# A hybrid decoder layer: six of eleven blocks of the second down pair by seven products, two of them made behind the next block's first

## The chip, the cores and the metric

One core of one Trainium2 chip runs the whole kernel in one launch. The metric is device time in microseconds, the median of several executions. One execution was also taken by the hardware profiler; all rows quoted below are from it. Engines: PE is TensorE, DVE is VectorE, ACT is ScalarE, POOL is GpSimd, SP is SyncE, which here only issues DMAs.

## The reference

One layer of a decoder for 256 rows of 2048 channels. Only its last step matters here:

```
def hybrid_layer(x, g_mix, w_in, ..., w_gu, w_down, rel_bias):
    ...                                    # three attention branches, merged with gates
    x = x + merged @ w_out
    h2 = rmsnorm(x, g_ffn)
    gu = h2 @ w_gu
    x = x + (jax.nn.silu(gu[..., :D_FF]) * gu[..., D_FF:]) @ w_down
    return x
```

All values are float32. With D_FF = 5632 the down projection multiplies a (256 x 5632) activation by a (5632 x 2048) weight.

## The kernel before

Each float32 operand of a large product is split into a high part (rounded to the matmul's format, `fp32r`, by a cast on ACT) and a low part (what is left, by a subtraction on DVE); the product is three matmuls, high by high, high by low and low by high (`product`, lines 177 to 179; the split is line 109, in `split`, called by `parts`). One weight tile is a "quarter" of 512 KB: 128 partitions x 2 k-tiles x 512 columns. Its split parts go into the tiles `w_hi` and `w_lo`, of which there are five each; a sixth cast must wait until PE is done with the first.

The down projection is made in two pairs of column blocks, 2 x 512 columns each, by `down_pair`. The second call, whose code changes, makes the last 1024 columns. In a pair the inner dimension is eleven blocks of 512. A block is a 2 x 2 matrix (two halves of rows of the activation, t, and two halves of the inner dimension, kh) times a 2 x 2 matrix of quarters (kh, n), and it is made in one of two ways:

- plainly (`rest`, one quarter a step): four quarters, each split once, 12 matmuls of 128x512 a quarter, 48 in all;
- by seven products (`seven`) instead of eight, with sums of quarters: seven splits, six matmuls each, 42 in all. f1 multiplies b11; f5 multiplies u = b11 + b12; f6 multiplies u + b22; f7 multiplies b12 + b22; f3 is b22, f2 is b21; f4 multiplies u + b21. f1, f5, f6 and f7 collect in PSUM tiles of their own for all blocks of the pair, and `combine` adds them into the output at the end; f2, f3 and f4 go straight into the output tiles (`own`).

In the second pair of the kernel before, five blocks are made by sevens: 4, 6, 8, 3 and 5, in this order; six are plain. u is one buffer (`bufs=1`): b11 + b12 and then + b22 are adds on DVE (lines 1203 and 1207), and the + b21 is a DMA that adds, issued by POOL (line 1229); b12 + b22 is such a DMA too (line 1223). In the last block the + b21 is a DVE add (line 1227). Where `seven` yields True, the caller puts one plain step in (`rest`): four for each block, after f1, f5, f6 and f7. The last plain block closes the pair.

The activation's sums that a block by sevens needs exist for blocks 4, 6 and 8 from the first pair. For blocks 3 and 5, `sums_again` loads the activation once more through POOL's queue (line 1154), makes four sums on DVE (lines 231 to 236) and splits them into the room of a plain block that is done (`again = {0: 3, 1: 5}`).

The weights' loads are issued by SP in its program's order (line 319); `w_raw` has four buffers for plain steps, `g_raw` four for blocks by sevens. The order on each engine is set by a scheduler in the build, except where `keep_in_program_order` holds an instruction in the place in which the code has it. PSUM: the pair's tiles `z`, `v` and two of `tr` are the output's (`own`), `ps` and `qs` (two each) hold f1, f5, f6 and f7.

Of the kernel before, what the change touches and what calls it, by code (L numbers as in the profile page):

```python
# [10 lines left out]
F32 = mybir.dt.float32  # L11
# [3 lines left out]
ALU = mybir.AluOpType  # L15
# [4 lines left out]
P = 128  # L20
# [10 lines left out]
NB = 512  # L31
# [25 lines left out]
def hybrid_block(ctx: ExitStack, tc: tile.TileContext, x, w_in, w_branch, w_out, w_gu, w_down, rel_bias,  # L57
                 onehot, extra, across, factors, out):
    nc = tc.nc
# [22 lines left out]
    def pool(stack, name, side, bufs=1):  # L82
        return stack.enter_context(tc.tile_pool(name=name, bufs=bufs, side=side, reuse_waits="tile"))
# [31 lines left out]
    def block(w, k, col0):  # L115

        return w[col0 // NB, k // 2]
# [30 lines left out]
    def project(acts, k0, w, row0, nk, col0, ps=None, done=0, there=(), last=1):  # L148


        ps = ps or banks()
        held = []
        for k, w_hi, w_lo in weights(w, row0, done, nk, col0, there):
            if k:
                advance(stages)
            if k % 2 == 0 and k:
                advance(slow_stages)
            held.append((k, w_hi, w_lo))
            if k < nk - last or k == nk - 1:
                for t in range(NT):  # L160
                    for kk, hi, lo in held:
                        product(ps[t], *acts.plain(t, k0 + kk), hi, lo, kk == 0, kk == nk - 1)
                held = []
        return ps
# [75 lines left out]
    class Sums:  # L240
# [22 lines left out]
        def form(self, f, c, j):  # L263
            if f in SUM_AT:
                kh, t = SUM_AT[f]
                return [x[:, 2 * kh + j, t * P:(t + 1) * P] for x in self.s[c]]
            return self.plain(*{1: (0, 4 * c + j), 2: (0, 4 * c + 2 + j), 4: (1, 4 * c + 2 + j)}[f])
# [48 lines left out]
    def load(w, k, col0, pl=None):  # L316

        raw = pl.tile([P, 2, NB], F32, name="g_raw", bufs=6 if pl is gx else 4) if pl else wpool.tile([P, 2, NB], F32, name="w_raw", bufs=4)
        (nc.sync.dma_start if w is w_down else fetch)(raw, block(w, k, col0))
        return raw  # L320
# [25 lines left out]
    def quarter(acts, w, kh, col0):  # L346
        return [load(w, 4 * c + 2 * kh, col0, gx) for c in acts.wc]

    def begin_pair(acts, w, colA, colB):

        b11, b12 = (quarter(acts, w, 0, col0) for col0 in (colA, colB))
        p11 = [parts(b) for b in b11]
        u = [gx.tile([P, 2, NB], F32, name="u") for _ in acts.wc]
        for a, b, d in zip(b11, b12, u):
            nc.vector.tensor_add(d, a, b)  # L355
        b21 = quarter(acts, w, 1, colA)
        return p11, b12, u, b21, [parts(b) for b in (u if by_banks(w) else b21)]
# [515 lines left out]
    def gate_col(c, b):  # L873
        return 3 * NH * HD + b * D + c * NB

    def pair_of(kind, what):
        if kind == "qk":
            return hs, w_in, what * NB, NH * HD + what * NB
        if kind == "gates":
            return hs, w_in, gate_col(*what[0]), gate_col(*what[1])  # L880
        if kind == "vv":
            return hs, w_in, V0 + what[0] * NB, V0 + what[1] * NB
        if kind == "vg":
            return hs, w_in, V0 + what[0] * NB, gate_col(*what[1])
# [15 lines left out]
    ahead = None  # L900
    for (kind, what), after in zip(units, units[1:] + [(None, None)]):
# [9 lines left out]
        if kind in ("qk", "gates", "vv", "vg"):  # L911
            ps, ahead = project_pair(*pair_of(kind, what), ahead, nxt, others is in_turn)
            if others is in_turn:
                turn.reverse()
        else:
            ps = project(h, 0, w_in, 0, KT, V0 + what * NB if kind == "v" else gate_col(*what),
                         *((ps0, 4, there) if (kind, what) == ("v", 0) else ()))
            ahead = begin_pair(*nxt) if nxt else None
# [57 lines left out]
    for c in range(4):  # L976
        ms = [half_kb() for _ in range(NT)]
        for b, (k0, nk) in enumerate(((0, H_A), (H_A, H_B), (H_A + H_B, H_C))):
# [3 lines left out]
            ps = project(o, k0, w_branch, k0 * P, nk, c * NB)  # L982
            if (c, b) == (3, 2):
# [4 lines left out]
                ahead = begin_pair(ms_sums.part(WC[:1]), w_out, NB, 0)  # L988
# [38 lines left out]
    gd = pool(ctx, "gd", "right", 4)  # L1027
# [22 lines left out]
    WD = (4, 6, 8)  # L1050
# [81 lines left out]
    pd = pool(ctx, "pd", "left")  # L1132
# [30 lines left out]
    def down_pair(c0, mine, spare, queues, sevenths, again={}):  # L1163


        own = dict(zip(((0, 0), (1, 0), (0, 1), (1, 1)), mine()))
# [7 lines left out]
        def into(ps, lhs, wh, wl, last=False, half=None):  # L1174
            for j in range(2):
                product(ps, *lhs(j), wh[:, j], wl[:, j], id(ps) not in begun, last and j == 1, half)
                begun.add(id(ps))
# [12 lines left out]
        def form(ps, f, c, src, last=False):  # L1190
            wh, wl = parts(src)
            into(ps, lambda j: a.form(f, c, j), wh, wl, last)

        def seven(c, f1, f5, f6, f7, last):
            def quarter(kh, n):
                return load(w_down, 4 * c + 2 * kh, c0 + n * NB, gd)

            b11 = quarter(0, 0)
            form(f1, 1, c, b11, last)
            yield bool(again)  # L1200
            b12 = quarter(0, 1)
            u = gd.tile([P, 2, NB], F32, name="u", bufs=1)
            tc.keep_in_program_order(nc.vector.tensor_add(u, b11, b12))  # L1203
            form(f5, 5, c, u, last)
            yield bool(again)
            b22 = quarter(1, 1)
            nc.vector.tensor_add(u, u, b22)
            if not again:
                form(f6, 6, c, u, last)
                yield  # L1210
                nc.vector.tensor_add(b12, b12, b22)
                form(f7, 7, c, b12, last)
                yield
                form(own[0, 1], 3, c, b22)
                yield
                b21 = quarter(1, 0)
                form(own[0, 0], 2, c, b21)
                yield
                nc.vector.tensor_add(u, u, b21)
                form(own[1, 0], 4, c, u)  # L1220
                yield
                return
            nc.gpsimd.dma_start(b12, b22, accum_op=ALU.add)
            form(f6, 6, c, u, last)
            b21 = quarter(1, 0)
            if last:
                tc.keep_in_program_order(nc.vector.tensor_add(u, u, b21))
            else:
                nc.gpsimd.dma_start(u, b21, accum_op=ALU.add)
            yield True  # L1230
            form(own[0, 1], 3, c, b22)
            yield
            form(own[0, 0], 2, c, b21)
            yield
            form(f7, 7, c, b12, last)
            yield True
            form(own[1, 0], 4, c, u)
            yield

        def combine(f1, f5, f6, f7):  # L1240

# [14 lines left out]
        def by_sevens():  # L1256
            f = spare()
            apart.extend(f[:1] if again else ())
            for c in sevenths:
                yield from seven(c, *f, c == sevenths[-1])  # L1260
            yield from combine(*f)

        sevens = by_sevens()
# [34 lines left out]
        return [acc2.tile([P, NB], F32, name=n) for n in "zv"] + [tr.tile([P, NB], F32, name="tr") for _ in range(2)]  # L1298

    down_pair(0, in_acc, elsewhere, (nc.scalar, nc.gpsimd), WD)  # L1300
    down_pair(2 * NB, elsewhere, in_acc, (nc.sync, nc.scalar), WD + (3, 5), {0: 3, 1: 5})


_INS = ["x", "w_in", "w_branch", "w_out", "w_gu", "w_down", "rel_bias"]
# [33 lines left out]
```

## Time and profile before

| what | value |
|---|---|
| median of three runs | 1336.18 us (1335.87 to 1337.33) |
| the profiled execution | 1335.64 us |
| its span from the first to the last instruction | 1333.9 us |
| PE busy | 1327.6 us |
| DVE busy | 1176.0 us |
| ACT busy | 946.2 us |
| POOL busy | 132.4 us |
| DMA, mean over the span | 267 GB/s |

The profiled execution is the one that every duration below comes from; between its span and its time lie 1.7 us, and it stands 0.54 us under the median. PE shows as busy nearly throughout. A matmul's own record is longer (0.38 us) than the time to the next one's start, since matmuls are pipelined, so times between starts are what counts for PE, and the same holds for the records of ACT and DVE to a smaller degree. The second pair's matmuls begin at 1222.67 us of the span. In a timeline row the columns are: start, duration, engine, line, operation, output and inputs by the program's names, form, and in brackets the idle time of the engine before it with what ended it.

### The profile page before, as it was taken

The page shows a single profiled execution, that of the slowest core. Times are in us where ns is not written, and L with a number is a line of the kernel's source. Part 1 is how long each engine was busy: PE and PEld are TensorE (multiplying, and loading weights), DVE is VectorE, ACT ScalarE, POOL GpSimd, SP SyncE. Part 2 cuts the span into 40 slices and gives each one's busy share as a digit, 9 for nine tenths or more (in the row PEclk, how much of TensorE's full clock was granted, in tenths as well). Part 3 has the DMA queues.
Part 4 walks back from the last instruction along what each step waited for, and adds up shares of the span by engine and source line. Part 5 has one row for each costly group of instructions (what it writes and reads, how often), then busy time and mean ns, then how long its engine had stood idle before and what let it go on. Part 6 is the DMA issues. An engine that isn't in the chain of part 4 may idle for free.

```text
span 1333.9 us, 17798 instructions
## 1 busy us (share of the span) xinstructions
PE 1327.6 (100%) x6243; PEld 1158.4 (87%) x6243; DVE 1176.0 (88%) x1261; ACT 946.2 (71%) x1216; POOL 132.4 (10%) x197
## 2 busy tenths in 40 slices
PE   9999999999999999999999999999999999999998
PEld 6888888888888888888888888888888888888887
DVE  7978898989888897888999999998889997998887
ACT  6786867788777776546778778777877876665563
POOL 1100110001111111110210000001000001001010
PEclk9999999999999999999999999999999999999999
DMA  9987977897789878887988889889899977789893
GB/s 359 307 284 243 263 211 256 254 282 215 263 267 289 275 245 276 297 304 255 284 314 268 273 257 275 234 260 302 280 286 278 270 222 256 250 276 303 269 273 96
DMA packets 119793, 355.75 MB, mean 267 GB/s; under 512 B 32864, under 2 KB 34584, under 8 KB 119704
## 3 DMA queue, kind: packets, MB, share of 16 engines
q1 hardware_dynamic: 77016, 277.45, 57.9%
q0 software_dynamic: 20272, 70.81, 22.7%
q10 hardware_dynamic: 22416, 6.36, 3.0%
q8 instruction: 49, 0.80, 0.2%
q14 instruction: 40, 0.33, 0.1%
HBM read 294.26 MB, written 14.70 MB: 232 GB/s over the span
## 4 chain that ended last, share of the span: by engine, by line
PE 97%; DVE 1%; DMA 1%; ACT 0%; issue 0%; SPq 0%; DVEq 0%; ACTq 0%
PE qs L178 12%; PE qs L177 12%; PE qs L179 12%; PE ps L178 11%; PE ps L179 11%; PE ps L177 11%; PE z L177 4%; PE z L179 4%; PE z L178 4%; PE v L177 3%; PE v L179 3%; PE v L178 3%; PE tr L179 1%; PE tr L177 1%; PE tr L178 1%; PE tr L210 1%
## 5 line engine op out<-in xcount | busy, mean ns | idle before, releaser
L109 DVE TENSOR_TENSOR w_lo<-w_raw,w_hi 128x1024 fp32r<-128x1024 f32 x298 | 361.5, 1222 | 45.6 <-ACT w_hi L109 44.4
L109 ACT CAST w_hi<-w_raw 128x1024 fp32r<-128x1024 f32 x298 | 309.3, 1047 | 95.8 <-PE qs L179 26.0
L109 ACT CAST w_hi<-g_raw 128x1024 fp32r<-128x1024 f32 x220 | 227.0, 1050 | 105.7 <-PE qs L179 32.9
L109 DVE TENSOR_TENSOR w_lo<-g_raw,w_hi 128x1024 fp32r<-128x1024 f32 x220 | 262.7, 1223 | 19.4 <-ACT w_hi L109 16.9
L109 ACT CAST w_hi<-u 128x1024 fp32r<-128x1024 f32 x165 | 172.1, 1049 | 116.9 <-DVE u L1203 21.3
L109 DVE TENSOR_TENSOR w_lo<-u,w_hi 128x1024 fp32r<-128x1024 f32 x165 | 199.8, 1224 | 45.0 <-ACT w_hi L109 40.1
L178 PE MATMUL qs<-w_lo,h_hi 128*128 128x512 f32 x348 | 132.6, 381 | 0.0
L179 PE MATMUL qs<-w_hi,h_lo 128*128 128x512 f32 x348 | 132.1, 379 | 0.0
L178 PE MATMUL ps<-w_lo,h_hi 128*128 128x512 f32 x336 | 128.0, 381 | 0.5 <-DVE w_lo L109 0.5
L179 PE MATMUL ps<-w_hi,h_lo 128*128 128x512 f32 x336 | 127.4, 380 | 0.1
L177 PE MATMUL qs<-w_hi,h_hi 128*128 128x512 f32 x348 | 127.4, 382 | 0.0
L177 PE MATMUL ps<-w_hi,h_hi 128*128 128x512 f32 x336 | 123.1, 382 | 0.0
L406 POOL DMA_DIRECT2D u<-g_raw x47 | 40.9, 871 | 375.6 <-DVE w_lo L109 311.2
L177 PEld LDWEIGHTS qs<-w_hi,h_hi 128*128 128x128 f32 x348 | 65.7, 189 | 9.5 <-ACT sc L339 0.4
L178 PEld LDWEIGHTS qs<-w_lo,h_hi 128*128 128x128 f32 x348 | 65.8, 189 | 9.2
L179 PEld LDWEIGHTS qs<-w_hi,h_lo 128*128 128x128 f32 x348 | 65.8, 189 | 9.2
L178 PEld LDWEIGHTS ps<-w_lo,h_hi 128*128 128x128 f32 x336 | 63.5, 189 | 9.9 <-DVE w_lo L109 1.3
L179 PEld LDWEIGHTS ps<-w_hi,h_lo 128*128 128x128 f32 x336 | 63.5, 189 | 9.9 <-DVE h_lo L109 1.1
L177 PEld LDWEIGHTS ps<-w_hi,h_hi 128*128 128x128 f32 x336 | 63.3, 189 | 9.2 <-ACT h_hi L109 0.6
L355 DVE TENSOR_TENSOR u<-g_raw 128x1024 f32<-128x1024 f32 x47 | 57.4, 1223 | 10.3 <-DMA g_raw<-in_w_gu 7.6
L344 DVE TENSOR_TENSOR u<-u,g_raw 128x1024 f32<-128x1024 f32 x47 | 55.5, 1220 | 0.0
L400 POOL DMA_DIRECT2D g_raw<-g_raw x21 | 18.2, 865 | 255.5 <-DMA g_raw<-in_w_in 104.3
(442 smaller groups left out, 2982.3 us busy)
## 6 DMA issues: line engine op xcount, KB each, us to landing
w_raw<-in_w_in SPq DMA_DIRECT2D x103, 512.0 KB, 7.1
g_raw<-in_w_in SPq DMA_DIRECT2D x88, 512.0 KB, 6.1
g_raw<-in_w_gu SPq DMA_DIRECT2D x88, 512.0 KB, 6.1
w_raw<-in_w_gu SPq DMA_DIRECT2D x88, 512.0 KB, 6.5
w_raw<-in_w_down SPq DMA_DIRECT2D x56, 512.0 KB, 4.9
u<-g_raw POOLq DMA_DIRECT2D x51, 512.0 KB, 6.1
w_raw<-in_w_branch SPq DMA_DIRECT2D x32, 512.0 KB, 4.8
g_raw<-in_w_down SPq DMA_DIRECT2D x32, 512.0 KB, 5.1
```

The costliest lines, as they stand in the source:

```text
L109: cast, rest = nc.scalar.copy(hi, src), nc.vector.tensor_sub(lo, src, hi.bitcast(F32))
L177: nc.tensor.matmul(ps, ah, wh, start=start, stop=False, **how)
L178: nc.tensor.matmul(ps, ah, wl, start=False, stop=False, **how)
L179: nc.tensor.matmul(ps, al, wh, start=False, stop=stop, **how)
L210: nc.tensor.transpose(pt[:, i, :], src[:, i * P:(i + 1) * P], ident)
L344: tc.keep_in_program_order(nc.vector.tensor_add(d, d, a))
L355: nc.vector.tensor_add(d, a, b)
L400: nc.gpsimd.dma_start(d, a, accum_op=ALU.add)
L406: nc.gpsimd.dma_start(d, a, accum_op=ALU.add)
```

## The change

Block 7 joins the blocks made by sevens: 4, 6, 8, 3, 5, 7, so five blocks stay plain. Its activation sums are made again in the room of block 2. A new generator, `sevens_apart`, takes the place of `seven` in the second pair: f7 and f4 of a block are put off (`due`) and made right after f1 of the next block. For the third and the fifth of the six blocks (8 and 5), u and b12 stand not in their usual buffers but in the room of block 4's activation sums (`a_shi4`, `a_slo4`), which are read no more by then; b12 is loaded there directly (line 1241). The plain steps are placed anew: before f5 (`ahead`), before f6 (`amid`) and before f3 (`behind`), 16 in all: three each for blocks 4, 6, 8 and 3, and two each for blocks 5 (none before f3) and 7 (none before f5). The first block's u + b21 is now a DVE add, like the last one's.

```
-            yield bool(again)
...                                 (seven: the first pair's form alone stays)
+        def sevens_apart(f1, f5, f6, f7):
+            due = []
+            def quarter(c, kh, n):
+                return load(w_down, 4 * c + 2 * kh, c0 + n * NB, gd)
+            def overdue():
+                while due:
+                    ps, f, c, src, last = due.pop(0)
+                    form(ps, f, c, src, last)
+                    yield
+            for i, c in enumerate(sevenths):
+                last = c == sevenths[-1]
+                ahead, amid, behind = i < 5, True, i < 4 or last
+                b11 = quarter(c, 0, 0)
+                if i and i % 2 == 0:
+                    b12, u = (pd.tile([P, 2, NB], F32, name=f"a_s{n}{sevenths[0]}") for n in ("hi", "lo"))
+                    nc.sync.dma_start(b12, block(w_down, 4 * c, c0 + NB))
+                else:
+                    b12, u = quarter(c, 0, 1), gd.tile([P, 2, NB], F32, name="u", bufs=1)
+                form(f1, 1, c, b11, last)
+                yield
+                yield from overdue()
+                tc.keep_in_program_order(nc.vector.tensor_add(u, b11, b12))
+                yield ahead
+                form(f5, 5, c, u, last)
+                b22 = quarter(c, 1, 1)
+                tc.keep_in_program_order(nc.vector.tensor_add(u, u, b22))
+                nc.gpsimd.dma_start(b12, b22, accum_op=ALU.add)
+                yield amid
                 form(f6, 6, c, u, last)
+                b21 = quarter(c, 1, 0)
+                if i and not last:
+                    nc.gpsimd.dma_start(u, b21, accum_op=ALU.add)
+                yield behind
+                if last or not i:
+                    tc.keep_in_program_order(nc.vector.tensor_add(u, u, b21))
                 form(own[0, 1], 3, c, b22)
                 yield
                 form(own[0, 0], 2, c, b21)
                 yield
-            form(f7, 7, c, b12, last)
-            yield True
-            form(own[1, 0], 4, c, u)
-            yield
+                due += [(f7, 7, c, b12, last), (own[1, 0], 4, c, u, False)]
+                if last or not i:
+                    yield from overdue()
...
-            for c in sevenths:
-                yield from seven(c, *f, c == sevenths[-1])
+            if again:
+                yield from sevens_apart(*f)
+            else:
+                for c in sevenths:
+                    yield from seven(c, *f, c == sevenths[-1])
...
-    down_pair(2 * NB, elsewhere, in_acc, (nc.sync, nc.scalar), WD + (3, 5), {0: 3, 1: 5})
+    down_pair(2 * NB, elsewhere, in_acc, (nc.sync, nc.scalar), WD + (3, 5, 7), {0: 3, 1: 5, 2: 7})
```

Two places show how the order moves. The first is ACT's, from the cast for f6 of one block to the cast for f5 of the next. Before, between blocks 3 and 5: the casts are f6's (from u), a plain step's (`w_raw`), f3's, f2's, f7's (`g_raw` each), a plain step's, f4's (u), f1's of block 5, a plain step's, and f5's (the new u).

```order
L109 CAST w_hi_11742<-u_11708 128x1024
L109 CAST w_hi_11757<-w_raw_11755 128x1024
L109 CAST w_hi_11773<-g_raw_11738 128x1024
L109 CAST w_hi_11783<-g_raw_11752 128x1024
L109 CAST w_hi_11793<-g_raw_11706 128x1024
L109 CAST w_hi_11805<-w_raw_11803 128x1024
L109 CAST w_hi_11821<-u_11708 128x1024
L109 CAST w_hi_11833<-g_raw_11831 128x1024
L109 CAST w_hi_11845<-w_raw_11843 128x1024
L109 CAST w_hi_11865<-u_11863 128x1024
```

Now, between blocks 5 and 7: f6's (`a_slo4` is u here), f3's, f2's, f1's of block 7, f7's of block 5 (`a_shi4` is b12), f4's of block 5, the copy of the sum of f1, f5's of block 7, a plain step's, f6's of block 7.

```order
L109 CAST w_hi_11833<-a_slo4_11744 128x1024
L109 CAST w_hi_11846<-g_raw_11811 128x1024
L109 CAST w_hi_11856<-g_raw_11843 128x1024
L109 CAST w_hi_11871<-g_raw_11866 128x1024
L109 CAST w_hi_11881<-a_shi4_11743 128x1024
L109 CAST w_hi_11891<-a_slo4_11744 128x1024
L339 COPY sc_12005<-ps_11191 128x512
L109 CAST w_hi_11902<-u_11870 128x1024
L109 CAST w_hi_11918<-w_raw_11916 128x1024
L109 CAST w_hi_11934<-u_11870 128x1024
```

Three plain steps' casts that stood between f6's and the next f5's are gone, and f1 of the next block has moved ahead of f4.

The second place is DVE's, from the low part of f4 to that of the next block's f5. Before, between blocks 8 and 3: low parts of f4, of f1, of a plain step, then the add that makes the new u, then f5's low part.

```order
L109 TENSOR_TENSOR w_lo_11667<-u_11547,w_hi_11666 128x1024
L109 TENSOR_TENSOR w_lo_11679<-g_raw_11676,w_hi_11678 128x1024
L109 TENSOR_TENSOR w_lo_11691<-w_raw_11688,w_hi_11690 128x1024
L1203 TENSOR_TENSOR u_11708<-g_raw_11676,g_raw_11706 128x1024
L109 TENSOR_TENSOR w_lo_11711<-u_11708,w_hi_11710 128x1024
```

Now, between blocks 3 and 5: the low part of f4, then the four sums of `sums_again` for block 7 with a plain step's low part among them, then the add, the low part of the activation's sums and f5's low part.

```order
L109 TENSOR_TENSOR w_lo_11767<-u_11600,w_hi_11766 128x1024
L231 TENSOR_TENSOR a_raw_11723<-a_raw_11723 128x2x128
L109 TENSOR_TENSOR w_lo_11784<-w_raw_11781,w_hi_11783 128x1024
L234 TENSOR_TENSOR a_raw_11723<-a_raw_11723 128x2x128
L235 TENSOR_TENSOR a_raw_11723<-a_raw_11723 128x2x128
L236 TENSOR_TENSOR a_raw_11723<-a_raw_11723 128x2x128
L1247 TENSOR_TENSOR a_slo4_11744<-g_raw_11741,a_shi4_11743 128x1024
L109 TENSOR_TENSOR a_lo2_6423<-a_raw_11723,a_hi2_6422 128x1024
L109 TENSOR_TENSOR w_lo_11802<-a_slo4_11744,w_hi_11801 128x1024
```

f1's low part has moved ahead of f4's, and a set of sums has come between f4 and the new u.

More of the change, by code (lines that the diff above doesn't have):

```diff
@@ L1204, in seven @@
             form(f5, 5, c, u, last)
-            yield bool(again)
+            yield
             b22 = quarter(1, 1)
             nc.vector.tensor_add(u, u, b22)
-            if not again:
-                form(f6, 6, c, u, last)
-                yield
-                nc.vector.tensor_add(b12, b12, b22)
-                form(f7, 7, c, b12, last)
-                yield
+            form(f6, 6, c, u, last)
+            yield
+            nc.vector.tensor_add(b12, b12, b22)
+            form(f7, 7, c, b12, last)
@@ new lines, in seven @@
+            yield
+            form(own[0, 1], 3, c, b22)
+            yield
+            b21 = quarter(1, 0)
+            form(own[0, 0], 2, c, b21)
+            yield
+            nc.vector.tensor_add(u, u, b21)
+            form(own[1, 0], 4, c, u)
+            yield
+        def sevens_apart(f1, f5, f6, f7):
[6 more added lines that the diff above has]
+                    form(ps, f, c, src, last)
+                    yield
+            for i, c in enumerate(sevenths):
[8 more added lines that the diff above has]
+                form(f1, 1, c, b11, last)
+                yield
+                yield from overdue()
[6 more added lines that the diff above has]
+                yield amid
+                form(f6, 6, c, u, last)
+                b21 = quarter(c, 1, 0)
[4 more added lines that the diff above has]
+                    tc.keep_in_program_order(nc.vector.tensor_add(u, u, b21))
@@ L1214, in seven @@
                 form(own[0, 1], 3, c, b22)
                 yield
-                b21 = quarter(1, 0)
                 form(own[0, 0], 2, c, b21)
                 yield
-                nc.vector.tensor_add(u, u, b21)
-                form(own[1, 0], 4, c, u)
[L1221 to L1229, printed above, removed]
@@ L1230, in seven @@
-            yield True
[L1231 to L1238, printed above, removed]
+                due += [(f7, 7, c, b12, last), (own[1, 0], 4, c, u, False)]
+                if last or not i:
+                    yield from overdue()
         def combine(f1, f5, f6, f7):
```

## The prediction

> **What bounds the kernel now.** I read the page's busy shares and chain first, then the engines by stretch, then the order of time around the second down pair (PE there from 1222.67 us).
>
> ```profile
> span 1333.9 us, 17798 instructions
> PE 1327.6 (100%) x6243; PEld 1158.4 (87%) x6243; DVE 1176.0 (88%) x1261; ACT 946.2 (71%) x1216; POOL 132.4 (10%) x197
> PE 97%; DVE 1%; DMA 1%; ACT 0%; issue 0%; SPq 0%; DVEq 0%; ACTq 0%
> ...
> 1223.00:1320.00 97.00, 97.00 (x451) 84.94 (x450) 83.42 (x83) 58.66 (x59) 7.94 (x10) 1.00 0.81 244
> 1320.00:1334.00 14.00, 10.36 (x54) 9.05 (x52) 6.52 (x13) 0.00 (x0) 0.00 (x0) 0.99 0.22 76
> ...
> PE ps L178 <- DVE w_lo L109: 0.5, 2, 0.3
> ```
>
> The two stretch rows give length, then busy time of PE, PEld, DVE, ACT and POOL, the clock, the DMA share and GB/s. PE is busy for all 97.00 us of the pair's main stretch at full clock; the last row is its longest wait for a split, 0.3 us in one piece. So the kernel is bound by its matmuls, and fewer matmuls are worth their time as long as the splits stay ahead of PE. DVE (83.42 of 97 us) and the DMA engines (0.81) are close behind.
>
> How far ahead are they? Product names: f1 to f7 as in the code. PE, one block of the pair:
>
> ```profile
> 1265.41 0.38 PE L177 MATMUL ps<-w_hi,a_shi 128*128 128x512 f32 x1
> ...
> 1269.29 0.38 PE L177 MATMUL qs<-w_hi,a_shi 128*128 128x512 f32 x1
> ...
> 1279.65 0.38 PE L177 MATMUL v<-w_hi,a_1hi 128*128 128x512 f32 x1
> ...
> 1284.83 0.38 PE L177 MATMUL ps<-w_hi,hi 128*128 128x512 f32 x1
> ```
>
> These are the first matmuls of f5, f6 and f4 of block 8 and of f5 of block 3. From f5 to f5 lie 42 matmuls of a block and four plain steps of 12: 90 in 19.42 us, 0.2158 us each. Now the other side, which makes the operand that f5, f6 and f4 share (u): ACT, then DVE and POOL.
>
> ```profile
> 1260.32 1.05 ACT L109 CAST w_hi<-u 128x1024 fp32r<-128x1024 f32 x1 [2.51 <-DVE u L1203]
> ...
> 1265.35 1.05 ACT L109 CAST w_hi<-u 128x1024 fp32r<-128x1024 f32 x1 [3.04 <-DVE u L1207]
> ...
> 1273.96 1.06 ACT L109 CAST w_hi<-u 128x1024 fp32r<-128x1024 f32 x1 [1.69 <-DMA u<-g_raw]
> 1274.92 1.04 ACT L109 CAST w_hi<-g_raw 128x1024 fp32r<-128x1024 f32 x1
> 1276.18 1.05 ACT L109 CAST w_hi<-w_raw 128x1024 fp32r<-128x1024 f32 x1 [0.23 <-PE z L179]
> 1279.80 1.06 ACT L109 CAST w_hi<-u 128x1024 fp32r<-128x1024 f32 x1 [2.56 <-DVE u L1203]
> ...
> 1284.49 1.05 ACT L109 CAST w_hi<-u 128x1024 fp32r<-128x1024 f32 x1 [2.71 <-DVE u L1207]
> 1285.44 1.04 ACT L109 CAST w_hi<-w_raw 128x1024 fp32r<-128x1024 f32 x1
> ```
>
> ```profile
> 1263.68 0.42 DVE L231 TENSOR_TENSOR a_raw<-a_raw 128x256 f32<-128x256 f32 x1
> 1264.02 1.22 DVE L1207 TENSOR_TENSOR u<-u,g_raw 128x1024 f32<-128x1024 f32 x1
> 1265.15 0.42 DVE L234 TENSOR_TENSOR a_raw<-a_raw 128x256 f32<-128x256 f32 x1
> ...
> 1266.42 1.23 DVE L109 TENSOR_TENSOR w_lo<-u,w_hi 128x1024 fp32r<-128x1024 f32 x1
> ...
> 1275.06 1.23 DVE L109 TENSOR_TENSOR w_lo<-u,w_hi 128x1024 fp32r<-128x1024 f32 x1 [0.59 <-ACT w_hi L109]
> 1276.20 1.22 DVE L109 TENSOR_TENSOR w_lo<-g_raw,w_hi 128x1024 fp32r<-128x1024 f32 x1
> 1277.33 1.22 DVE L109 TENSOR_TENSOR w_lo<-w_raw,w_hi 128x1024 fp32r<-128x1024 f32 x1
> 1278.47 1.22 DVE L1203 TENSOR_TENSOR u<-g_raw 128x1024 f32<-128x1024 f32 x1
> ...
> 1267.95 0.85 POOL L1229 DMA_DIRECT2D u<-g_raw x1 [6.36 <-DVE w_lo L109]
> ...
> DMA to landing us min/median/max: 5.8/5.9/7.2
> ```
>
> The u of a block runs in series. From the cast for f5 to the cast for f6: 1279.80 to 1284.49, 4.69 us (low part, a plain step's low part, u += b22). From f6's cast to f4's: 1265.35 to 1273.96, 8.61 us, of which the adding DMA is 5.9 (last row: the four of this pair). From f4's cast to the next f5's: the low part starts 1.10 later, takes its 1.14, and from the next u's add to its cast are 1.33 (1278.47 to 1279.80): 3.57 if nothing else of DVE stands between. Together 16.87 us a block. PE spends 19.42 on it now, so the feed is ahead: f4's high part is ready at 1275.02, PE takes it at 1279.65.
>
> **The change part by part.** *Matmuls.* Block 7 goes from 48 to 42: 6 x 0.2158 = 1.30 us off PE.
>
> *The loop of u against PE.* This is where I expect the time to go. The same 16 plain steps are now spread over six blocks, three to a block and fewer at the end; f7 and f4 of a block stand behind f1 of the next, and the next u waits on DVE until f4's low part is made. In PE's order the changed kernel has 244 matmuls from f5 of block 6 to f5 of block 5 (three turns), 52.65 us; the feed needs 3 x 16.87 = 50.61, and between blocks 3 and 5 DVE also has four sums and a plain low part ahead of the next u: 0.34 (1263.68 to 1264.02) + 1.14 + 1.27 (1265.15 to 1266.42, three) = 2.75. That is 53.36, so 0.71 more than PE. From f5 of block 5 to f5 of block 7 only 54 matmuls are left (one plain step in place of four), 11.65 us against 16.87: short by 5.22. In block 7, f5 to f6 has 18 matmuls, 3.88 us against 4.69: 0.81; and the first matmul of the plain step behind f6 stands right behind f6's first, while its cast starts 0.95 later (1284.49 to 1285.44): 0.95 - 0.22 = 0.73. Then casts of loaded quarters follow, and the feed gains again.
>
> Against this stands the lead at the start. There are five w_hi buffers; f1 of block 6 needs the one whose last matmul stands 32 ahead of that block's f5, 6.91 us. From there: wake-up 0.23, f1's cast to its low part 1.28 (1274.92 to 1276.20), that one's turn 1.13, the add to the cast 1.33, the cast 1.05: 5.02. Lead 1.9 us. After three turns 1.9 - 0.71 = 1.19 are left. Sum of stalls with DMAs of 5.9: 5.22 - 1.19 + 0.81 + 0.73 = 5.57.
>
> *The adding DMAs.* The trace of before has this DMA at 5.8 to 7.2, and the one that adds b22 into b12 between these:
>
> ```profile
> L1223 POOL DMA_DIRECT2D g_raw<-g_raw x5: 847/856/890, 1218.8 to 1299.4; - x5
> ...
> DMA to landing us min/median/max: 5.0/7.6/8.2
> ```
>
> Four of them are in the loop. I take three as the median and one at 7.2, since a third load of an activation block now shares POOL's queue: +1.3. The ends are all four at 7.6 (+6.8) and the last at 5.0 (-0.9; a gain in the three turns ahead is lost, as the five buffers hold f4 of block 3 to 24 matmuls less 0.23 and a cast, 3.9 us, and so block 5's f5 to 3.9 + 3.88 - 6.32 = 1.46).
>
> A row against a rule: this DMA takes 5.9 us, the adding one into b12 never less than 5.0. The Trainium skill (DMA: Bandwidth & Descriptors, section "Anatomy of one DMA — SWDGE (gpsimd) path") gives a GpSimd-issued DMA as about 2.0 us plus its bytes at 436 GB/s, an estimate of 3.2 us for 512 KB; by it the sum would be about +1.3 us and not +5.6. The trace disagrees for DMAs that add.
>
> *DVE, ACT.* DVE gets three more splits, two more u adds, the first block's u += b21 that a DMA made before (1.14 a turn, six), four sums and one split of the activations (2.8): about 10 us in all; ACT four casts. DVE idles 13.6 of the 97 us and ACT 38, so by quantity it fits; what is late of it is in the loop above. Between nothing and 3 us more, taken as nothing.
>
> *DMA queues.* SP issues the same number of loads; two go into dead sums' room and wait for PE (done by then) or an earlier cast, with the loads behind them on SP's queue waiting along. In before, SP's waits (30 us for low parts alone) cost ACT nothing here:
>
> ```profile
> ACT w_hi L109 <- DMA u<-g_raw: 3.1, 2, 1.7
> ...
> SPq L319 <- DVE w_lo L109: 29.4, 12, 4.6
> ```
>
> No row of ACT waits for a load in this stretch. I take 0; from below there is no gain in it, from above one late load, a landing beyond its cover, some 3 us. POOL has two DMAs more, of 0.9 us issue each, between waits of 6 to 12 us: 0. The f7 products now have longer for their DMA; nobody waited for it: 0.
>
> Sum: 5.57 + 1.3 - 1.30 = +5.6 us. The profiled execution took 1335.64, so 1341.2; the median of the runs shown is 0.54 above it, so **1341.8**. Ends: 5.22 - 0.9 - 1.46 + 1.54 - 1.30 = +3.1 (1339.3) and 5.57 + 6.8 - 1.30 = +11.1 (1347.3).
>
> **The rivals.** (a) *Only the matmuls count:* 1334.9, faster by 0.10%, which is within 0.2%, about what a measurement of this kernel can tell from no change. For it: PE was covered in every row, with 4.6 us of lead at f4. Against: it needs the last turn of the loop to shrink from 16.87 to under 13, and DMA and casts alone are 5.9 + 3.1. (b) *The adding DMAs are the bottleneck:* they meet loads that PE's stalls bunch up, all at 7.6 or more: 1345 to 1347. For it: the DMA share is 0.81 and b12's took 7.6. Against: three of four u's took 5.8 to 5.9 beside two loads. (c) *They land like the quickest plain load:* the shortest landing of any DMA into a g_raw buffer in this stage is 3.5 us:
>
> ```profile
> DMA to landing us min/median/max: 3.5/5.7/8.5
> ```
>
> The last turn is then 2.4 shorter, and the lead at block 5's f5 at its cap: 5.22 - 2.4 - 1.46 + 1.54 - 1.30 = +1.6, 1337.8. This is also what the rule above comes to. Against it are the adding DMAs' own rows. (d) *The clock drops.* PE's gaps will be the first of more than 0.3 us in this pair, up to 25 matmuls (5.39 us) against 8.61, 3.2 us. All rows have the clock at 1.00, and 0.99 in the last 14 us. If PE ran at half speed for as long as such a gap, 3.4 us more, 1345.2. The Trainium skill (TensorE: Matmul & The Clock Gate, section "What's actually happening") says the clock halves after an idle window of about 3.4 us; by that the gaps stay just short of it.
>
> **How the numbers follow.** The forecast has 0.67 (1339.3 to 1344.5), (a) 0.08, (b) 0.10, (c) 0.11, (d) 0.04. The range leaves out (a), most of (b) and part of (c) and (d): 1338.0 to 1345.0. Within 0.2% (1333.5 to 1338.9) are (a) less a remnant and most of (c): 0.15; faster by over 0.2% needs a gain that no row shows: 0.03; slower by over 0.2%: 0.82.
>
> **What would show it.** In the changed kernel PE should have gaps, first about f5 of block 5, the largest ahead of f4 of block 5 (v, some 2 to 3 us, behind an ACT wait for the DMA that fills the second u), then about 1 us at f5 of block 7 and 0.7 behind its f5 and f6; some 7 us of idle PE in all. Wrong would be: no gap over 0.3 us (then a turn is shorter than I read it), gaps in the first three turns as large as in the fourth (then the DMAs are slower), or a clock below 1.

## The result, and the profile after

The changed kernel takes 1344.18 us (median of six runs, 1342.88 to 1346.4) against 1336.51 for the kernel before on the same chip: 7.7 us slower, ratio 1.0056, 95% interval 1.0043 to 1.0069. The profiled execution took 1343.85 us, its span is 1342.1, 8.2 more than before. First the page's span, busy shares and chain:

```profile
span 1342.1 us, 17801 instructions
PE 1329.3 (99%) x6237; PEld 1156.3 (86%) x6237; DVE 1184.8 (88%) x1272; ACT 949.5 (71%) x1220; POOL 134.2 (10%) x199
...
PE 93%; DVE 3%; DMA 2%; issue 1%; ACT 1%; SPq 0%; POOL 0%; ACTq 0%; DVEq 0%; POOLq 0%
```

The chain leaves PE more often than before (93 against 97%). The pair's main stretch, with the columns as in the prediction:

```profile
1223.00:1320.00 97.00, 91.14 (x410) 76.50 (x409) 80.49 (x82) 54.35 (x56) 9.37 (x12) 1.00 0.85 249
```

And PE's waits in the window of this pair (1223 to 1342 us), each with its total, how often, and the longest:

```profile
PE v L177 <- ACT w_hi L109: 1.9, 1, 1.9
PE tr L177 <- ACT w_hi L109: 1.8, 4, 0.5
PE ps L177 <- ACT w_hi L109: 1.6, 3, 0.9
PE z L177 <- ACT w_hi L109: 0.5, 1, 0.5
```

Six matmuls fewer in the program, but 41 fewer in this stretch: PE now waits, and always for a high part. DVE and ACT are busy for less of this window than before (80.49 and 54.35 us; part of their work now comes behind it), so neither is full; the clock is 1.00. Where PE waits, in the order of time (its rows with an idle time):

```profile
1259.17 0.48 PE L177 MATMUL ps<-w_hi,a_shi 128*128 128x512 f32 x1 [0.38 <-ACT w_hi L109]
1260.12 0.70 PE L177 MATMUL tr<-w_hi,hi 128*128 128x512 f32 x2 [0.46 <-ACT w_hi L109]
...
1296.72 0.48 PE L177 MATMUL ps<-w_hi,hi 128*128 128x512 f32 x1 [0.33 <-ACT w_hi L109]
1297.67 0.70 PE L177 MATMUL tr<-w_hi,a_hi 128*128 128x512 f32 x2 [0.47 <-ACT w_hi L109]
1302.35 0.48 PE L177 MATMUL tr<-w_hi,hi 128*128 128x512 f32 x1 [0.47 <-ACT w_hi L109]
1309.84 0.48 PE L177 MATMUL v<-w_hi,a_hi 128*128 128x512 f32 x1 [1.94 <-ACT w_hi L109]
1310.16 0.38 PE L178 MATMUL qs<-w_lo,hi 128*128 128x512 f32 x1
...
1313.36 0.48 PE L177 MATMUL ps<-w_hi,a_hi 128*128 128x512 f32 x1 [0.88 <-ACT w_hi L109]
1314.31 0.48 PE L177 MATMUL z<-w_hi,a_hi 128*128 128x512 f32 x1 [0.46 <-ACT w_hi L109]
...
1318.97 0.70 PE L177 MATMUL tr<-w_hi,a_hi 128*128 128x512 f32 x2 [0.45 <-ACT w_hi L109]
```

These are f5 of block 8 and the plain step behind it, f5 of block 5 and the plain step behind it, f3 of block 5 (behind its f6), f4 of block 5 (the longest), f5 of block 7 and the plain step behind it, and the plain step behind f6 of block 7. The idle time in brackets understates a wait, since the records of matmuls overlap. So below I add up, over all matmuls of the pair, what each starts later than 0.2158 us after the one before it ("late starts"): 0.10 us in the kernel before, 8.96 in the changed one. 8.96 - 0.10 - 1.30 for six matmuls is 7.56; the other 0.6 of the 8.2 us of span lies ahead of the pair (late starts there 15.90 against 15.35). That is code which the change leaves as it was; over all the profiles of this case its late starts vary from 14.8 to 16.7 us, so the span of a single profile is no finer than that.

The other side, the casts from u on ACT (`a_slo` is u in blocks 8 and 5), for f5, f6 and f4 of blocks 6, 8, 3 and 5 and for f5 and f6 of block 7:

```profile
1238.69 1.06 ACT L109 CAST w_hi<-u 128x1024 fp32r<-128x1024 f32 x1 [1.26 <-DVE u L1247]
...
1243.39 1.06 ACT L109 CAST w_hi<-u 128x1024 fp32r<-128x1024 f32 x1 [2.70 <-DVE u L1251]
...
1254.52 1.05 ACT L109 CAST w_hi<-u 128x1024 fp32r<-128x1024 f32 x1 [3.70 <-DMA u<-g_raw]
...
1258.07 1.05 ACT L109 CAST w_hi<-a_slo 128x1024 fp32r<-128x1024 f32 x1 [0.61 <-DVE a_slo L1247]
...
1263.75 1.04 ACT L109 CAST w_hi<-a_slo 128x1024 fp32r<-128x1024 f32 x1 [3.68 <-DVE a_slo L1251]
...
1272.38 1.05 ACT L109 CAST w_hi<-a_slo 128x1024 fp32r<-128x1024 f32 x1 [2.84 <-DMA a_slo<-g_raw]
...
1275.93 1.04 ACT L109 CAST w_hi<-u 128x1024 fp32r<-128x1024 f32 x1 [1.56 <-DVE u L1247]
...
1280.80 1.05 ACT L109 CAST w_hi<-u 128x1024 fp32r<-128x1024 f32 x1 [1.94 <-DVE u L1251]
...
1289.35 1.05 ACT L109 CAST w_hi<-u 128x1024 fp32r<-128x1024 f32 x1 [2.75 <-DMA u<-g_raw]
...
1295.62 1.05 ACT L109 CAST w_hi<-a_slo 128x1024 fp32r<-128x1024 f32 x1 [0.17 <-DVE a_slo L1247]
...
1300.31 1.04 ACT L109 CAST w_hi<-a_slo 128x1024 fp32r<-128x1024 f32 x1 [2.69 <-DVE a_slo L1251]
...
1308.74 1.04 ACT L109 CAST w_hi<-a_slo 128x1024 fp32r<-128x1024 f32 x1 [3.59 <-DMA a_slo<-g_raw]
...
1312.27 1.04 ACT L109 CAST w_hi<-u 128x1024 fp32r<-128x1024 f32 x1 [1.99 <-DVE u L1247]
...
1316.93 1.06 ACT L109 CAST w_hi<-u 128x1024 fp32r<-128x1024 f32 x1 [2.67 <-DVE u L1251]
```

Every one of these casts waits for u itself, the f4 casts for the adding DMA. ACT's casts waited for u before, too; what is new is that PE then waits for the casts. From f5 to f5 the four turns take 19.38, 17.86, 19.69 and 16.65 us, 73.58 in all. Two things in them are to be seen elsewhere. The landing times of the four DMAs that add into u (POOL, line 1257), from the view of that line:

```profile
DMA to landing us min/median/max: 5.7/5.9/8.1
```

Those of the six that add into b12 (line 1252):

```profile
DMA to landing us min/median/max: 4.4/6.9/10.1
```

And two of DVE's rows in the second turn:

```profile
1256.74 1.22 DVE L1247 TENSOR_TENSOR a_slo<-g_raw,a_shi 128x1024 f32<-128x1024 f32 x1
1257.87 1.22 DVE L109 TENSOR_TENSOR lo<-a_raw,hi 128x1024 fp32r<-128x1024 f32 x1
```

The 8.1 is the first turn's: from f6's cast to f4's are 11.13 us there, against 8.63, 8.55 and 8.43 in the other three. In the second turn the low part of the made-again activations (`lo`, 1.14 us of DVE's time) stands between the new u's add and the low parts that f6's u must wait for: 5.68 from f5's cast to f6's, against 4.69 before.

### The profile page after: what moved, and what is told of

Its sections match the earlier page's. It is cut to its first block, busy times and chain, and to the rows that moved or that the text cites. A ratio compares the mean times of both kernels' runs of the same rounds, so it can differ in the third digit from the quotient of the medians.

```text
span 1342.1 us, 17801 instructions
## 1 busy us (share of the span) xinstructions
PE 1329.3 (99%) x6237; PEld 1156.3 (86%) x6237; DVE 1184.8 (88%) x1272; ACT 949.5 (71%) x1220; POOL 134.2 (10%) x199
## 4 chain that ended last, share of the span: by engine, by line
PE 93%; DVE 3%; DMA 2%; issue 1%; ACT 1%; SPq 0%; POOL 0%; ACTq 0%; DVEq 0%; POOLq 0%
PE qs L178 12%; PE qs L179 12%; PE qs L177 12%; PE ps L178 11%; PE ps L179 11%; PE ps L177 11%; PE z L177 4%; PE z L178 4%; PE z L179 4%; PE v L177 2%; PE v L179 2%; PE v L178 2%; DVE w_lo L109 1%; PE tr L210 1%; DMA a_slo<-g_raw 1%
## 5 line engine op out<-in xcount | busy, mean ns | idle before, releaser
L109 DVE TENSOR_TENSOR w_lo<-w_raw,w_hi 128x1024 fp32r<-128x1024 f32 x294 | 356.0, 1219 | 44.2 <-ACT w_hi L109 43.0
L109 ACT CAST w_hi<-w_raw 128x1024 fp32r<-128x1024 f32 x294 | 305.1, 1047 | 92.9 <-PE qs L179 26.5
L109 DVE TENSOR_TENSOR w_lo<-g_raw,w_hi 128x1024 fp32r<-128x1024 f32 x222 | 264.7, 1220 | 19.2 <-ACT w_hi L109 16.8
L109 ACT CAST w_hi<-u 128x1024 fp32r<-128x1024 f32 x162 | 168.9, 1049 | 107.1 <-PE ps L179 21.7
L109 DVE TENSOR_TENSOR w_lo<-u,w_hi 128x1024 fp32r<-128x1024 f32 x162 | 195.7, 1222 | 41.5 <-ACT w_hi L109 36.2
```

Source lines behind the costliest of these rows:

```text
L109: cast, rest = nc.scalar.copy(hi, src), nc.vector.tensor_sub(lo, src, hi.bitcast(F32))
```

## The experiments

Times are in us. "Over" is the kernel's median less the median of the kernel before on the same chip.

| run | time | over | ratio, 95% interval |
|---|---|---|---|
| changed kernel | 1344.18 | +7.7 | 1.0056 [1.0043, 1.0069] |
| five_deferred | 1335.96 | +0.2 | 1.0002 [0.9992, 1.0011] |
| six_inplace | 1352.51 | +16.8 | 1.0125 [1.011, 1.014] |
| dve_all | 1338.52 | +2.8 | 1.0021 [1.0007, 1.0035] |
| u_early | 1339.72 | +4.0 | 1.0033 [1.002, 1.0046] |
| steps_late | 1340.09 | +4.2 | 1.0031 [1.002, 1.0042] |
| no_sums7 | 1341.87 | +6.0 | 1.0048 [1.0029, 1.0067] |
| u_early_steps_late | 1335.95 | 0.0 | 0.9994 [0.9982, 1.0006] |
| early_late_dve6 | 1334.53 | -1.4 | 0.9984 [0.9972, 0.9996] |
| dve_6 | 1343.35 | +7.8 | 1.0056 [1.0041, 1.0071] |
| dve_5 | 1342.93 | +7.3 | 1.0059 [1.0042, 1.0075] |
| b12_dve | 1347.1 | +11.5 | 1.0085 [1.007, 1.01] |
| dve_6_5 | 1342.18 | +6.4 | 1.0046 [1.0031, 1.006] |

The theory: PE is held by the turn of u, a series of casts, DVE adds and an adding DMA that no longer fits beside the fewer matmuls of a turn. Its rivals: the new order by itself, DVE's added work, slow DMAs under the added loads.

**The two halves of the change.** *five_deferred* has the new order with the old five blocks and four plain steps in each (the comments in these cuts name the place):

```
-                ahead, amid, behind = i < 5, True, i < 4 or last
+                ahead, amid, behind = True, True, True
...
-                yield                       # after f2
+                yield True
-    down_pair(..., WD + (3, 5, 7), {0: 3, 1: 5, 2: 7})
+    down_pair(..., WD + (3, 5), {0: 3, 1: 5})
```

> The new order (f7 and f4 behind the next block's first, two u buffers in turn) with the five blocks of before and four plain steps a block. Theory 'the loop' (u's series of adds, casts and the adding DMA, 16.9 to 19.7 us a block, against PE's matmuls of the same turn): PE again has 90 matmuls, 19.4 us, in each turn, so no gaps worth naming: 0 +- 1 us against before. Rival 'the order itself costs' (work put behind the next block's first makes the feed late): some 3 to 8 us slower than before, as in the changed kernel.

It takes the time of the kernel before; its late starts over the pair are 0.17 us. Where a turn has 90 matmuls, the order, the second u and the dead sums' room cost nothing. *six_inplace* is the other half, from the kernel before: six blocks in the old order with one u, the 16 plain steps spread 3, 3, 3, 3, 2, 2.

```
-            yield bool(again)               # after f1
+            yield bool(again) and not last
-            yield True                      # after f6
+            yield c != 5
-            yield True                      # after f7
+            yield
-    down_pair(..., WD + (3, 5), {0: 3, 1: 5})
+    down_pair(..., WD + (3, 5, 7), {0: 3, 1: 5, 2: 7})
```

> Six blocks by sevens, but in the order of before: f7 and f4 of a block stay in it, one u buffer; plain steps 3, 3, 3, 3, 2, 2. 'The loop': PE's turn is as short as in the changed kernel, while the turn of u is longer by a low part of f1 (1.1 us) and has fewer products between f6 and f4 (f3, f2, f7, one step at most): slower than the changed kernel, 10 to 17 us over before. 'The order itself costs': better than the changed kernel, under +5 us.

Six blocks with too few steps a turn cost 16.8 us; the deferred order takes half of that back. Late starts are 18.4 us, the longest waits 3.2 us at f5 of block 5 and 1.8 at an f4. So what costs is the sixth block's taking of plain steps, not where f7 and f4 stand.

**Shortening the series.** *dve_all* replaces the adding DMA into u by a DVE add (1.14 us of DVE) in every block:

```
-                if i and not last:
-                    nc.gpsimd.dma_start(u, b21, accum_op=ALU.add)
                 yield behind
-                if last or not i:
-                    tc.keep_in_program_order(nc.vector.tensor_add(u, u, b21))
+                tc.keep_in_program_order(nc.vector.tensor_add(u, u, b21))
```

> The changed kernel with u + b21 as a DVE add in all six blocks, no adding DMA into u (four DMAs of 512 KB less, four DVE adds of 1.14 us more). 'The loop': the 5.9 to 8.1 us of landing go from each turn, the wait ahead of f4 of block 5 (2.1 us) goes, what is left is f5 of block 7 and short ones: 3 to 5 us faster than the changed kernel, +2 to +5 over before. 'DVE has no room' (the quantity of DVE work is the bound): 3 to 5 us slower than the changed kernel.

4.9 us less than the changed kernel's +7.7, though DVE has four adds more. DVE's quantity isn't the bound. *u_early* moves one line: the next u's add goes ahead of f7 and f4 of the block before.

```
+                tc.keep_in_program_order(nc.vector.tensor_add(u, b11, b12))
                 yield from overdue()
-                tc.keep_in_program_order(nc.vector.tensor_add(u, b11, b12))
```

> The changed kernel with one line moved: the add that makes the next block's u stands ahead of f7 and f4 of the block before, not behind. No instruction more or less. 'The loop': f4's cast no longer stands in series with the next u (3.5 us from f4's cast to f5's become 2, the four sums stand behind the add as well), so some 4 to 6 us faster than the changed kernel, +1 to +4 over before. 'DMA load' (the extra adding DMAs and loads delay the feed) and 'DVE has no room': no change against the changed kernel, +7 to +8 over before.

The same loads, adds and DMAs, and 3.7 us come back, a little under the 4 to 6 expected. The DVE rows between blocks 5 and 7 show why. First the changed kernel's, then those of u_early:

```profile
1309.82 1.22 DVE L109 TENSOR_TENSOR w_lo<-a_slo,w_hi 128x1024 fp32r<-128x1024 f32 x1 [2.67 <-ACT w_hi L109]
1310.96 1.22 DVE L1247 TENSOR_TENSOR u<-g_raw 128x1024 f32<-128x1024 f32 x1
```

```profile
1302.65 1.22 DVE L1246 TENSOR_TENSOR u<-g_raw 128x1024 f32<-128x1024 f32 x1
1303.78 1.22 DVE L109 TENSOR_TENSOR w_lo<-a_shi,w_hi 128x1024 fp32r<-128x1024 f32 x1
1305.42 1.23 DVE L109 TENSOR_TENSOR w_lo<-a_slo,w_hi 128x1024 fp32r<-128x1024 f32 x1 [0.42 <-ACT w_hi L109]
```

In the changed kernel the add that makes the new u stands behind f4's low part. In u_early it is done before f7's and f4's low parts, so it no longer waits for the adding DMA through f4. The four stretches from f4's cast to the next f5's fall from 3.55, 3.55, 6.27 and 3.53 us to 2.85, 2.85, 1.90 and 0.95. So a DVE instruction stood in the series that need not be there.

**More matmuls in the short turns.** *steps_late* takes two plain steps out of block 4, whose turn has cover to spare, and gives one each to blocks 5 and 7:

```
-                ahead, amid, behind = i < 5, True, i < 4 or last
+                ahead, amid, behind = i > 0, True, i > 0
```

> The changed kernel with the same 16 plain steps placed otherwise: one in the first block (4), three in each of the five others, so that the turn from f5 of block 5 to f5 of block 7 has three of them (78 matmuls, 16.8 us) and not one. 'The loop': the short turn's 5.2 us go, the first block loses lead in exchange (1.9 us at most), some 3 to 5 us faster than the changed kernel, +2 to +5 over before. 'DMA load' and 'DVE has no room': the same transfers and the same DVE work, no change, +7 to +8.

3.5 us less than the changed kernel. *no_sums7* leaves out the third set of activation sums; block 7 multiplies block 5's in its place.

```
+        if c == 5:
+            a.s[7] = a.s[5]
-    down_pair(..., {0: 3, 1: 5, 2: 7})
+    down_pair(..., {0: 3, 1: 5})
```

> The changed kernel without the third set of activation sums: block 7's three products read block 5's sums instead, so the load, four sums and the split of block 7 are left out (2.75 us of DVE in the turn from block 3 to 5, one load of 512 KB). 'The loop': that turn is 2.8 us shorter, of which the five buffers let at most some 1.5 to 2.5 be kept as lead: 1.5 to 3 us faster than the changed kernel, the wait at f4 of block 5 stays near 2 us or shrinks to 1. 'DVE has no room': nearly the same gain. 'DMA load': under 1 us.

1.7 us less in time, 2.6 in span. Its third turn (f5 of block 3 to f5 of block 5) is 16.81 us against 19.69; the other three are within 0.1 of the changed kernel's. So the third set of sums costs its time in the turn in which it stands between f4's low part and the next u.

**Together.** *u_early_steps_late* has both edits of these names; *early_late_dve6* has them, and a DVE add into u in block 6, whose adding DMA was the late one:

```
-                if i and not last:
+                if i in (2, 3, 4):
                     nc.gpsimd.dma_start(u, b21, accum_op=ALU.add)
...
-                if last or not i:
+                if last or not i or i in (1,):
```

> The changed kernel with both: the next u's add ahead of f7 and f4, and one plain step in block 4, three in each other. 'The loop': a turn of u is 15 to 17 us against 16.8 of PE everywhere, gaps nearly gone: the 1.3 us of matmuls are left as gain or half of it, -1.3 to +1 against before. If the two gains did not add (one cause behind both): +2 to +3.

> As the kernel with both, and block 6's u + b21 as a DVE add (the one adding DMA that landed after 8.1 us instead of 5.9). 'The loop': no gap left: -1.3 +- 0.7 against before. If the landing time of that DMA did not matter: as the kernel with both, or 0.5 us slower by DVE's extra work.

The gains add up: the first is back at the time of the kernel before, the second is 1.4 us faster than it, about the six matmuls' 1.30, and 9.1 faster than the changed kernel. Its main stretch:

```profile
1223.00:1320.00 97.00, 97.00 (x451) 84.95 (x450) 90.46 (x92) 62.41 (x63) 8.51 (x11) 1.00 0.82 248
```

In the pair's window (1223 to 1335 us) the view of PE's waits has no row. PE is full again, with DVE at 90.46 of 97 us: what the change lacked was order, not capacity.

**Single DMAs.** Which turn cost what? *dve_6* and *dve_5* make only block 6's, or only block 5's, u + b21 on DVE (`i != 1`, or `i != 4`, in the condition of the DMA, and the reverse in that of the add); *dve_6_5* both; *b12_dve* keeps these DMAs and makes b12 + b22 on DVE:

```
-                nc.gpsimd.dma_start(b12, b22, accum_op=ALU.add)
                 yield amid
...
                 yield behind
+                nc.vector.tensor_add(b12, b12, b22)
```

> Only block 6's u += b21 goes to DVE; the other three stay adding DMAs. Its DMA was the one of the four that landed late (8.1 us). Theory of the turn: the first turn of u (19.38 us from f5's cast of block 6 to f5's of block 8) falls to the 17.19 it had where DVE made all of these adds, 2.2 us less, and since the lead was used up already in that turn, the time falls by as much: 5.0 to 6.0 us over the kernel before, about 1341.3, and the gap at f5 of block 8 goes. Rival, only the last turn counts (it is short of 5 us whatever stands ahead of it): the first turn's time goes into lead that the buffers cannot hold, and the time stays at that of the changed kernel, 7.7 over.

> Only block 5's u += b21 goes to DVE, in the last turn; the other three stay adding DMAs. Theory of the turn: the gap of 2.32 us ahead of f4 of block 5 goes, but the next u then waits in DVE's row, as where DVE made all of these adds (15.02 us from f5's cast of block 5 to that of block 7 against 16.65): 1.6 to 2.3 us less than the changed kernel, 5.4 to 6.1 over the kernel before, about 1341.7. Rival, the DMA is the whole of the last turn's shortage (8.43 us from f6's cast to f4's against 4.75 on DVE): 3.7 us less, 4.0 over the kernel before.

> b12 += b22 is made by DVE in place of the adding DMA, in all six blocks; u += b21 stays a DMA. Theory of the DMA load: the adding DMAs into u land late (5.7 to 8.1 us) because those into b12 (4.4 to 10.1) move beside them; without these the ones into u land in 5.0 to 5.9, and the time falls by up to 2.5 us, to 5 us over the kernel before. Theory of the turn in series: DVE has 1.14 us more in each of four turns, most of them between f5's low part and u += b22 or ahead of f4's, with no lead to hide them: 2 to 4.6 us more than the changed kernel, 10 to 12 over the kernel before, less what quicker DMAs give back in the first turn (2.3).

> u += b21 by DVE in blocks 6 and 5, DMAs in blocks 8 and 3. With block 6's alone the first turn did get 2.2 us shorter (17.21 against 19.38) and the gap at f5 of block 8 went, but the time did not fall: in that profile the wait of 2.0 us ahead of f4 of block 5 was followed by eight matmuls at 0.43 us each, half clock. Theory (turns add up, and the half clock hid the gain): without the DMA of block 5 no wait of 2 us is left, so all rows stay at clock 1.00, and both gains show: matmul starts 4.4 to 5.1 us late in sum over the pair (8.96 in the changed kernel, less 2.4 and less 1.5 to 2.2), 3.1 to 3.8 us over the kernel before, ratio 1.0023 to 1.0029. Rival (single adds on DVE give nothing; only the loads that all four free count): 6.0 to 7.5 us over, ratio 1.0045 to 1.0056, with the clock at 1.00 or not.

dve_6 went against my theory as I had sized it: no less time and 0.6 us less span, not about 2. dve_5 is hardly less by its median (7.3 over against 7.7, with a wide interval); its profiled execution, the fastest of its four, has a span 2.2 less. I then blamed a stretch at half clock in dve_6 (below), and dve_6_5 went against that: the clock was 1.00, and it came out at +6.4, the rival's figure. The rival's reason isn't needed for it, though: its late starts fell by 2.2 as its turns did, and in its profile the code ahead of the pair has 0.8 us more of them than the changed kernel's (16.66 against 15.90), which leaves the 1.3 or so that its time shows. The sum over all four turns explains the late starts of all of these runs. Starts of the casts for f5 of block 6 and of block 7, the time between, and the late starts:

| run | f5 of 6 | f5 of 7 | four turns | against changed | late starts | against changed |
|---|---|---|---|---|---|---|
| changed | 1238.69 | 1312.27 | 73.58 | | 8.96 | |
| no_sums7 | 1238.77 | 1309.64 | 70.87 | -2.71 | 6.25 | -2.71 |
| dve_6 | 1238.42 | 1311.62 | 73.20 | -0.38 | 8.60 | -0.36 |
| dve_5 | 1237.98 | 1310.01 | 72.03 | -1.55 | 7.42 | -1.54 |
| dve_6_5 | 1239.43 | 1310.81 | 71.38 | -2.20 | 6.77 | -2.19 |
| dve_all | 1237.97 | 1306.67 | 68.70 | -4.88 | 4.16 | -4.80 |
| b12_dve | 1237.76 | 1314.27 | 76.51 | +2.93 | 12.37 | +3.41 |
| u_early | 1237.60 | 1305.30 | 67.70 | -5.88 | 3.88 | -5.08 |

PE's late starts follow u's series within 0.1 us (in b12_dve f5 to f6 of block 7 is also 0.48 longer, 5.14 against 4.66, which makes +3.41 of +2.93; in u_early it is 0.78 longer, 5.44, which makes -5.10 of -5.88). The late starts are those of one profiled execution: u_early's is the fastest of its six (1337.70, median 1339.72), so its time shows less than its profile. PE has the same number of matmuls between those casts in all of them, so the lead at the start is the same, and what the series gains, PE gains. In dve_6 the first turn did fall by 2.17, to 17.21, and the next two grew by 0.90 and 0.88: block 8's adding DMA took 7.6 us now (10.34 from f6's cast to f4's), and the activations' low part moved from the second turn's f5-to-f6 into the third's (5.67 there against 4.87). Here is its second turn:

```profile
1255.63 1.05 ACT L109 CAST w_hi<-a_slo 128x1024 fp32r<-128x1024 f32 x1 [1.42 <-DVE a_slo L1247]
...
1260.50 1.05 ACT L109 CAST w_hi<-a_slo 128x1024 fp32r<-128x1024 f32 x1 [1.93 <-DVE a_slo L1251]
...
1270.84 1.04 ACT L109 CAST w_hi<-a_slo 128x1024 fp32r<-128x1024 f32 x1 [3.46 <-DMA a_slo<-g_raw]
...
1274.39 1.04 ACT L109 CAST w_hi<-u 128x1024 fp32r<-128x1024 f32 x1 [0.60 <-DVE u L1247]
```

So the gain was given back one turn later. The load of the activations is issued 1.3 us ahead of that DMA here (1261.83 and 1263.10 on POOL) and 7.0 ahead in the changed kernel (1259.39 and 1266.35); dve_6_5 has the same order (1262.84 and 1264.12), and that DMA took 7.4 us there. No run moves this load alone, so that it is what delays the DMA is not shown. For the adding DMAs' load on one another there are the rows of block 6 in the changed kernel:

```profile
1239.37 0.89 POOL L1252 DMA_DIRECT2D g_raw<-g_raw  x1 [14.00 <-DVE u L1247]
1246.00 0.88 POOL L1257 DMA_DIRECT2D u<-g_raw  x1 [5.75 <-DVE w_lo L109]
```

The first takes 10.1 us, so the DMA into u moves beside it for 3.5 us, and takes 8.1. The other three of the changed kernel are issued at most 0.2 us before b12's has landed, and take 5.7 to 5.9. The longest overlap of all the runs, some 4.5 us in block 6 of steps_late, goes with the longest landing, 8.9. b12_dve tries it: without the adding DMAs into b12 those into u land so (line 1257 there, too):

```profile
DMA to landing us min/median/max: 5.7/5.9/6.0
```

The late one is gone, so b12's DMA held the first one back. But DVE's six adds more cost more than that gives, and the kernel is 11.5 over, as the turn in series had it.

## Why the prediction was right, and where it was off

- *Mechanism.* The sign and the places were right, and the time lies in the range, 2.4 over the value: PE is bound by u's turns. It lies only 0.3 us inside the upper end, so the number was in part luck: the sizes of two turns were wrong (below), and 0.6 us of the loss lies in code ahead of the pair. The longest wait is ahead of f4 of block 5 (a start 2.32 us after the one before, forecast 2 to 3), then comes f5 of block 7 (1.26, so 1.04 late, forecast 1), and behind f5 and f6 of block 7 starts are 0.73 and 0.67 late (0.95 and 0.89 after the one before), forecast 0.7. The first gap came earlier than forecast, at f5 of block 8, and 1.8 us of the late starts lie ahead of f5 of block 5, where the forecast had none.
- *Matmuls, -1.30.* Right: where the waits are gone (early_late_dve6) 1.4 us remain.
- *The loop of u, +5.57, and the adding DMAs, +1.3.* These were mis-sized. Turns as forecast and measured: 16.87 and 19.38; 16.87 and 17.86; 19.62 and 19.69; 16.87 and 16.65. The third, with its 2.75 us for the sums, and the fourth, which carries the 5.22, were right within 0.3 us. The first was 2.51 over, all of it from f6's cast to f4's with the DMA of 8.1 (above the 7.2 of the rows of before); the second was over by 0.99, the activations' low part, which I had counted as quantity and not in the series. The four are 3.35 longer than forecast, less the 1.3 allowed for DMAs is 2.05: the late starts came to 7.56 net of matmuls, against 5.6.
- *The lead, 1.9.* With the measured turns: 73.58 + 4.66 to f6 of block 7, less 316 matmuls of 0.2158 (68.19), less 1.9, plus 0.73 behind that f6 is 8.9, against 8.96 late. So the lead held, but the first turn ate it, and I had 1.19 of it left for the last.
- *The wait row.* The row of PE's waits with 0.3 us that the prediction reads as the longest wait for a split is not of this pair: its two waits lie at 13 and 21 us of the span. In the pair's own window the view of the kernel before has no row at all, so that PE was covered there holds all the more.
- *DVE, ACT, 0; queues, 0.* Right in quantity (dve_all, early_late_dve6). What counted of DVE was its order.
- *Rivals.* (a) Only the matmuls: it needed a last turn under 13 us, and that took 16.65. (b) All adding DMAs at 7.6 or more: one of four was. (c) DMAs like a plain load: none of this kernel's into u was under 5.7 in the four runs whose rows I read for it (the changed one, dve_6, dve_5, b12_dve). The estimate of 3.2 us that follows from the Trainium skill's fit (DMA: Bandwidth & Descriptors, "Anatomy of one DMA — SWDGE (gpsimd) path") is not met by any of them. (d) The clock: 1.00 in the changed kernel's stretch, with its longest gap short of the 3.2 us forecast. The price of (d) was wrong as well: half speed for 3.2 us loses 1.6 us of work, not 3.4; in dve_6 eight starts at 0.43 us lost 1.7.

## What to carry to other kernels

Before a consumer is given less work per block, follow the buffer that it waits for once round, cast by cast, through every engine's queue in order, and set that series turn by turn against the consumer's work; the sum over the turns less the lead gave PE's loss here within 0.1 us, while busy shares (DVE 88%, ACT 71%) told nothing. Then shorten the series by order first: one DVE add put ahead of two low parts that it did not need was worth 3.7 us, and two steps moved to where the turn is short 3.5. A gain in one turn can be lost in the next when its transfers and in-order fill-ins move with it, so judge by the whole series, not by the gap that goes.

## What the hardware did that I had not expected

The clock went to half after waits shorter than I had thought safe. In dve_6, after 2.0 us of idle PE ahead of f4 of block 5, matmuls start 0.43 us apart, for 3.4 us; the stretch from 1310 to 1314 us (the clock is the third value from the end, 0.57), and then rows about its start:

```profile
1310.00:1314.00 4.00, 4.00 (x12) 2.85 (x11) 3.43 (x5) 1.99 (x2) 0.85 (x1) 0.57 0.45 131
```

```profile
1309.19 0.48 PE L177 MATMUL v<-w_hi,a_hi 128*128 128x512 f32 x1 [1.96 <-ACT w_hi L109]
...
1310.27 0.63 PE L178 MATMUL qs<-w_lo,hi 128*128 128x512 f32 x1
1310.70 0.63 PE L179 MATMUL qs<-w_hi,lo 128*128 128x512 f32 x1
```

The changed kernel has the same wait (1.94 us) at the same place, and its clock stayed at 1.00; six_inplace shows the half clock after waits of 3.2 and 1.8 us (0.50 from 1305 to 1307 us), b12_dve after one of 1.95.

The traces' records of the clock tell more. Every slow stretch among the pair's matmuls lasts 3.41 us, and where a trace has several drops they begin whole multiples of 3.41 us apart: in six_inplace at 1303.70, 1317.35 and 1351.49 us (4 and 10 times), in dve_6 at 1310.04 and 1340.76 (9 times), in b12_dve at 1311.95 and 1346.08 (10 times). This fits idle time being counted by windows on a fixed grid. Of all such windows that end ahead of the pair's last matmul, the four with the most idle PE in them, 1.95 us (b12_dve), 1.96 (dve_6), 2.01 and 3.21 (six_inplace), are the four that stand right ahead of a slow stretch; the next, with 1.62 us (no_sums7) and 1.57 (u_early), are not. By the grid of the changed kernel (its clock drops at 1343.06, behind its last matmul) a window ends at 1308.93, within its wait of 1.94 us, which leaves 1.04 us in one window and 0.91 in the next. That would explain why the same wait cost it no clock.

The Trainium skill (TensorE: Matmul & The Clock Gate, "What's actually happening") has the clock halve after an idle window of about 3.4 us, in free-running windows; the length of the slow stretches and their grid agree, a wholly idle window of that length was not needed here. In dve_6 the half clock cost little, since PE then waited for u anyway: dve_6's late starts follow its series within 0.1 us all the same.

A wait also costs a little beyond itself: the first one to three starts after it are 0.32 us apart and not 0.2158 (1309.84 to 1310.16 in the changed kernel), 0.1 us each. What causes that no run shows.
